# Four gate tiles moved behind the q, k, v projections, sample attention queued by groups, a shared buffer for its value sums, and weight splits on GpSimd beside a convolution

## The chip, the cores and the metric

The kernel runs on one core of a Trainium2 chip. The metric is the device time of one execution in microseconds. Five engines work side by side, each through its own instruction stream in a fixed order: TensorE (PE: matrix products, with PEld for its weight loads), VectorE (DVE), ScalarE (ACT), GpSimd (POOL) and SyncE (SP), which here only issues transfers. An instruction that waits holds up everything behind it on the same engine.

## The reference

One layer of a decoder with two gated branches, on 1024 prompt tokens and 8 sequences of 4 sample tokens, with width 1024 and all in float32:

```
h = RMSNorm(x);  z = h @ w_in -> GLU (2*512) | q, k, v (768 each) | gate_c (1024) | gate_a (1024)
A: GLU -> causal depthwise conv (width 31) -> LayerNorm over channels -> swish -> @ w_conv_out
B: attention in 3 groups of 4 heads, windows/dilations (128,1), (512,4), (2048,16) -> @ w_att_out
x = x + (sigmoid(gate_c) * A + sigmoid(gate_a) * B) @ w_out
x = x + SwiGLU(RMSNorm(x));  x = x + sigmoid(RMSNorm(x) @ w_ple_gate) * (p @ w_ple)
```

The prompt attends to itself. Each sample token attends to 129 or so keys of its sequence's cache (128 kept rows and the new ones) in each group; the caches are also copied to the outputs.

## The kernel before

**Tokens and products.** The 1056 tokens lie along the free dimension in three chunks of 352, features on the 128 partitions. Each large product is float32 made of three products of split operands: `mm3` (L118 to L120) multiplies high by high, high by low and low by high part for each of the 8 tiles along the contraction, so that a tile of 128 output columns for all tokens is 3 x 8 x 3 = 72 matmuls. They are `mm<-...` in the trace.

**Weights.** They come in slabs of 128 x 1024 in the order of a list. `stage` loads a slab (SyncE, L91), `prepare` makes its high part on ACT (`whi`, L101) and its low part on DVE (`wlo`, L102); two slabs are loaded ahead and one is split ahead. A scheduler places each engine's instructions by priority when the program is built; the splits have a raised priority.

**Phase 1** makes the embedding product, the first norm, and then 24 slabs of `w_in`: 8 for the GLU, 8 gate tiles of the conv branch and 8 gate tiles of the attention branch. A gate tile is evacuated from PSUM by ACT's sigmoid (L408) into a tile `et` (two buffers) and stored in DRAM (`gcd`, `gad`). While TensorE works on the gates, DVE makes the depthwise convolution: 31 taps for each of 4 channel tiles, each one operation on 128 x 1024 that reads `U` and `acc` (L332, L338). Then comes the LayerNorm over channels: DVE copies sums and squares of `acc` to `lt` (L366, L367), TensorE sums them over the channels with a matrix of ones (L369), and DVE and ACT normalise and apply swish (L372 to L386). The result is stored as `cd`.

**Phase 2** runs two pairs of heads, each through three groups: q, k and v products, scores (TensorE L707, DVE L712 with the running maxima `mcol`), then softmax and the products with v (L567 to L675). The q, k, v of the sample tokens are written to DRAM (`scr`). Behind pair 1, the pointwise product of the conv branch is made: three chunks of `cd` are loaded in halves into `et` (L758) and split (`split`, L123 on ACT, L124 on DVE), then for each of 8 output tiles the conv gate is loaded into an `et` (L765), three products of 12 matmuls are multiplied by it on DVE (L770) and the result is stored (L771).

**Sample attention** runs beside that, with (query, sequence, head) on the partitions and 8 keys a step. `sample_ops(g)` appends small steps to a queue `bg`. A key step loads 128 x 512 of the cache (L493, tile `kt`, four buffers), multiplies it by the query on GpSimd (L466) and sums over the head's 64 elements on DVE (L467); 16 such steps and one for new keys are followed by the softmax (`smax`). A value step loads the cache, multiplies by the weights on GpSimd (L477), reduces over the 8 keys on DVE (L484) and adds the 128 x 64 result to `oacc` (L487). All three groups are queued behind the conv product's code, and `pump` empties the queue there; the scheduler then interleaves the steps with the prompt's work by data and engine. `sample_out` combines the groups, transposes on TensorE (L516) and writes the sample columns of the attention product's operand (`ohi`, `olo`).

**The attention product** then needs `ohi` and, for each tile and chunk, the gates loaded from `gad` (L795). DVE multiplies its sum by the attention gate (L836), GpSimd adds the conv branch (L837), and the output product L854, the FFN, the embedding gate and the final norm follow.

What sets the order around the change: the slab list, the order of the code with the queue `bg` (and `bga` for softmax steps), and the number of steps that each `pump(n)` takes.

Of the kernel before, what the change touches and what calls it, by code (L numbers as in the profile page):

```python
# [20 lines left out]
TP = 1024            # prompt tokens  # L21
T = 1056             # prompt and sample tokens
NCH = 3              # token chunks
C = 352
CP = (352, 352, 320)  # prompt tokens in a chunk
KD = 8
FT = 22              # tiles of 128 hidden FFN columns
# [4 lines left out]
NB = (8, 8, 8)       # 128-query blocks in a group  # L32
SOFF = (0, 132, 261, 390)

# columns of the "vec" input
# [5 lines left out]
KEPT = (2, 3, 4, 5, 6)   # slabs of the last product that are used twice  # L41
# [3 lines left out]
def hybrid_layer(ctx: ExitStack, tc: tile.TileContext, I, O):  # L45
# [21 lines left out]
    # ---- weights: a slab is up to 8 tiles of 128 x 128, split into two float32r parts.  # L67
    # The slabs come in the order of their use, loads two and splits one ahead. ----
    order = [(I["w_ple"][i], 8) for i in range(2)]
    order += [(I["w_in"][i], 8) for i in range(42)]  # L70
# [13 lines left out]
    keep = [None]        # room for the slabs that are used twice  # L84
    last_act = [None]

# [7 lines left out]
    def prepare():  # L94
        if staged:
            st, n, kept = staged.popleft()
            p, b = (keep[0], len(KEPT)) if kept else (wp, 2)
            hi = p.tile([128, 8, 128], F32R, name="whi", tag="whi", bufs=b)
            lo = p.tile([128, 8, 128], F32R, name="wlo", tag="wlo", bufs=b)
            with tc.high_priority(offset=PRIO):  # L100
                last_act[0] = ac.activation(hi[:, :n, :], st[:, :n, :], AF.Copy)  # L101
                ve.tensor_tensor(lo[:, :n, :], st[:, :n, :], hi[:, :n, :].bitcast(F32), op=OP.subtract)  # L102
            ready.append((hi, lo))
            stage()
# [8 lines left out]
    def mm3(ps, w, ks, rhs):  # L113
        """ps = sum over k of w[k].T @ rhs[k]; ks: slab positions, rhs: (hi, lo) pairs."""
# [11 lines left out]
    def split_gain(hi, lo, x, g):  # L126
        """x times a gain per partition, split"""
        ac.activation(hi, x, AF.Copy, scale=g)
        ve.scalar_tensor_tensor(lo, x, g, hi.bitcast(F32), op0=OP.mult, op1=OP.subtract)

# [32 lines left out]
    J3 = (0, 128, 224)   # three (overlapping) runs of 128 tokens of a chunk  # L163

    def rstd_cols(p, sqs, n=float(D)):
        """1/sqrt(mean + eps) of the tokens of some chunks, tokens on the partitions;
        sqs: squares, summed over the feature tiles (a list: still to be summed)"""
# [11 lines left out]
        # first guess from the bits of v, then three Newton steps  # L179
# [9 lines left out]
    def rstd_rows(cols, i=0):  # L189
        """the same of the i-th chunk, tokens along the free dimension, on every partition (PSUM)"""  # L190
# [19 lines left out]
    # =====================================================================  # L210
    # phase 0 and 1: per-layer embedding product, first norm, gates, conv branch
    # =====================================================================
# [7 lines left out]
    ev = evs.enter_context(pool("ev"))          # evacuation buffers  # L220
# [7 lines left out]
    def mmtile(p):  # L228
        return p.tile([128, 512], F32, name="mm", tag="mm")
# [77 lines left out]
    def proj(evac, psp):  # L307
        """next tile of 128 columns of w_in, for all tokens"""
# [18 lines left out]
    def conv_ops(ct):  # L327
        """depthwise conv of one tile of 128 channels, as a list of small steps"""
# [31 lines left out]
    def layer_norm():  # L360
        """LayerNorm over the channels and swish"""
# [44 lines left out]
    for dst in gc_d + [d[:, 0] for d in ga_d]:  # L406
        et = et_tile()
        proj(lambda c, ps: ac.activation(et[:, c * C:(c + 1) * C], ps[:, :C], AF.Sigmoid), mm1)  # L408
        sy.dma_start(dst, et)
    pump(1000)  # L410
# [5 lines left out]
    # =====================================================================  # L416
    # phase 2: projections to q, k, v and attention, two heads at a time
    # =====================================================================
# [12 lines left out]
    # room for the tiles that are free early is taken last: the next phase's first loads go there  # L431
# [13 lines left out]
    def sample_ops(g):  # L445
# [4 lines left out]
        def load():  # L450
# [3 lines left out]
            st["q"] = a = sp.tile([128, 64], F32, name="sq", tag="sq", bufs=2)  # L454
            sy.dma_start(a, scr[g][0].rearrange("t (h d) -> (t h) d", d=64))
            for i, nm in ((1, "k"), (2, "v")):
                st[nm] = b = sp.tile([128, 4, 64], F32, name="sn" + nm, tag="sn" + nm, bufs=1)
                if g == 0:
                    for j in range(4):
                        sy.dma_start(b[32 * j:32 * j + 32],  # L460
                                     scr[g][i].rearrange("(n b) (h d) -> (b h) n d", n=4, d=64))
                else:
                    sy.dma_start(b[:, 0], scr[g][i].rearrange("t (h d) -> (t h) d", d=64))
# [12 lines left out]
        def v_part(vt, off, n):  # L476
            gp.tensor_tensor(vt, vt, st["s"][:, off:off + n, None].to_broadcast([128, n, 64]), op=OP.mult)  # L477
            if not st.get("o"):
                ve.tensor_reduce(oacc[:, g], vt.rearrange("p n d -> p d n"), axis=AX, op=OP.add)
                st["o"] = True  # L480
                return
            if n > 1:
                pr = sp.tile([128, 64], F32, name="pr", tag="pr", bufs=2)
                ve.tensor_reduce(pr, vt.rearrange("p n d -> p d n"), axis=AX, op=OP.add)  # L484
            else:
                pr = vt[:, 0]
            ve.tensor_tensor(oacc[:, g], oacc[:, g], pr, op=OP.add)  # L487
# [12 lines left out]
        bg.append(smax)  # L500
        steps("v", v_part)

    def sample_out():
# [13 lines left out]
        so = sp.tile([128, 2, 32], F32, name="so")  # L517
# [6 lines left out]
    def group_view(t, g):  # L524
        """prompt columns of t (in group order) seen in natural order: [p, u, r]"""
# [18 lines left out]
    def blocks(g):  # L544
        """(first query, first key, keys, first bias column) of the 128-query blocks"""
# [10 lines left out]
    def softmax_ops(pair, S, VT, mcol):  # L556
        st = {}

        def rows(g, hf):
            """maxima of a group as rows in token order, joined with the groups before"""  # L560
# [121 lines left out]
    for pair in range(2):  # L682
        S, VT = [], []
        mcol = ap_.tile([128, 3, 8, 2], F32, name="mcol", tag="mcol", bufs=2)
        for g in range(3):
# [4 lines left out]
            for i, nm in enumerate("qkv"):  # L690
                t = ap_.tile([128, T], F32, name=nm, tag=nm, bufs=1)
                qkv.append(t)
                proj(lambda c, ps: evac_group(t, g, c, ps, i), psm)
                if i == 1:
                    # scores with bias, and their maxima
# [4 lines left out]
                    for b0 in range(0, 8, 2):  # L700
                        # the two heads lie on different rows of the array: their products alternate
# [16 lines left out]
            # new rows of the caches  # L718
# [8 lines left out]
            # v with tokens on the partitions, and a column of ones for the denominators  # L727
# [11 lines left out]
            # q, k, v of the sample tokens, tokens on the partitions  # L739
            ps = misc()  # L740
            for i in range(3):
# [5 lines left out]
                         st[:, 1:, :])  # L747
        softmax_ops(pair, S, VT, mcol)
        pump(1000, bga)

    # pointwise product of the conv branch and its gate, while the last heads finish
# [20 lines left out]
    for g in range(3):  # L772
        sample_ops(g)
# [5 lines left out]
    # =====================================================================  # L779
    # attention product, gates, output product, first residual; FFN input  # L780
    # =====================================================================
# [32 lines left out]
    def to_input(p, c, m, gain):  # L814
        """the m-th feature tile of x1 to the next product's input (without the token's norm)"""
# [11 lines left out]
    for m in range(KD):  # L827
        if m % 4 == 0:
            w = slab()
        for c in range(NCH):  # L830
            s = slice(c * C, (c + 1) * C)
            ga = ga_next if c + m == 0 else ga_load(c, m)
            ps = mmtile(mm)
# [11 lines left out]
    # the first chunk's input goes to a place of its own, the others' to where their operands were  # L845
# [20 lines left out]
    # =====================================================================  # L866
    # FFN
    # =====================================================================
# [45 lines left out]
    # =====================================================================  # L914
    # PLE gate, last residual, final norm
    # =====================================================================
# [39 lines left out]
def _layout(inp):  # L956
# [12 lines left out]
    def tiles(w):  # L969
        """[K, M] -> [M / 128, 128 rows, K / 128, 128 columns]"""  # L970
# [3 lines left out]
    def slabs(w):  # L974
        """[K, M], K a part of 1024 -> [slab, 128 rows, tiles of a slab, 128 columns]"""
# [41 lines left out]
    # caches with (query, sequence, head) in front: the rows that a query reads  # L1017
# [11 lines left out]
    # constants of the shapes  # L1029
# [41 lines left out]
def _collect(r):  # L1071
# [7 lines left out]
    def prompt(a, n):  # L1079
        # [kv, pair, (e, d), n] in token order -> [n, kv, head, d]  # L1080
# [6 lines left out]
    # new rows: [g, kv, (n, b), (h, d)] -> [g, kv, b, n, h, d]  # L1087
# [4 lines left out]
    for g in (1, 2):  # L1092
        both = []
        for i, n in enumerate("kv"):
            old = r[f"o_{n}g{g}"].reshape(4, 8, 4, 127, 64).transpose(1, 3, 0, 2, 4)   # b, m, i, h, d
# [24 lines left out]
```

## Time and profile before

| | us |
|---|---|
| runs of the kernel before | 1720.19, 1723.10, 1723.71 (median 1723.1) |
| span of the profiled execution | 1721.7 |
| its TensorE busy / DVE / ACT / GpSimd | 1660.9 / 897.6 / 494.4 / 182.7 |

The profile describes one execution; its own time is the span, 1721.7 us, from the first to the last instruction, and the median of the runs is 1.4 us above it. Rows give a line of the kernel, an engine, an operation with the tiles it writes and reads, and times in microseconds unless marked ns; a duration triple is minimum, median and maximum in ns. "Idle before" is time that an engine stood still ahead of an instruction, with what ended the wait.

### The profile page before, as it was taken

Reading aid. Unit: us, or ns where it says so; the run is one execution under the profiler, and the core shown is the slowest. Engines: PE = TensorE matmul, PEld = TensorE weight load, DVE = VectorE, ACT = ScalarE, POOL = GpSimd, SP = SyncE. Lnnn points to the kernel's source line nnn. Section 1 sums busy time; section 2 is a strip of 40 time slices with the busy share of each in tenths; the row PEclk is TensorE's granted clock in tenths of the full one; section 3 lists DMA queues with packets and bytes.
Section 4 is the critical chain, followed back from the end, with each engine's and each line's share of the span. In section 5 each row is a group of like instructions: output and inputs, shape, how many; then the busy total and the mean of one; then the engine's idle time right before and its main releaser. Section 6 shows DMA issues by size and latency. Waiting matters only on the chain.

```text
span 1721.7 us, 25453 instructions
## 1 busy us (share of the span) xinstructions
PE 1660.9 (96%) x10554; PEld 1629.2 (95%) x10554; DVE 897.6 (52%) x1529; ACT 494.4 (29%) x890; POOL 182.7 (11%) x154
## 2 busy tenths in 40 slices
PE   7999999999999978799999999999999999999996
PEld 7999999999998868689999999999999999999996
DVE  7699995121225896874543323333233333337666
ACT  7211125322263225232322201221012111225552
POOL 3100000000003766460000000000000000000003
PEclk9999999999999999899999999999999999999998
DMA  8445554511203678681233323332111111111322
GB/s 306 170 136 172 184 182 156 179 48 55 70 29 116 187 262 269 205 289 50 72 107 120 99 70 99 118 115 74 50 62 37 36 52 62 39 35 51 118 87 108
DMA packets 69348, 201.14 MB, mean 117 GB/s; under 512 B 10096, under 2 KB 25264, under 8 KB 68144
## 3 DMA queue, kind: packets, MB, share of 16 engines
q1 hardware_dynamic: 66480, 153.50, 27.6%
q10 hardware_dynamic: 2752, 46.01, 8.1%
q8 instruction: 83, 1.36, 0.3%
q14 instruction: 33, 0.27, 0.1%
HBM read 171.17 MB, written 72.15 MB: 141 GB/s over the span
## 4 chain that ended last, share of the span: by engine, by line
PE 81%; DVE 6%; issue 6%; DMA 4%; POOL 1%; ACT 1%; SPq 0%; DVEq 0%; POOLq 0%; ACTq 0%
PE mm L118 26%; PE mm L120 25%; PE mm L119 25%; DVE pr L484 2%; DMA kt<-in_kg 2%; PE ps_s L707 1%; PE N L608 1%; POOL kt L466 1%; DVE oacc L487 1%; DMA ga<-gad 1%; DMA et<-gcd 1%; DVE sc L467 1%; PE misc L174 1%; POOL y L922 0%; PE ps_s L631 0%
## 5 line engine op out<-in xcount | busy, mean ns | idle before, releaser
L118 PE MATMUL mm<-hhi,whi 128*128 128x352 f32 x2480 | 807.4, 326 | 13.3 <-DVE et L770 7.7
L120 PE MATMUL mm<-hhi,wlo 128*128 128x352 f32 x2480 | 802.1, 324 | 0.0
L119 PE MATMUL mm<-hlo,whi 128*128 128x352 f32 x2480 | 799.3, 322 | 0.0
L118 PEld LDWEIGHTS mm<-hhi,whi 128*128 128x128 f32 x2480 | 467.2, 188 | 21.1 <-DVE et L770 10.7
L120 PEld LDWEIGHTS mm<-hhi,wlo 128*128 128x128 f32 x2480 | 468.1, 189 | 3.0 <-issue 2.7
L119 PEld LDWEIGHTS mm<-hlo,whi 128*128 128x128 f32 x2480 | 468.5, 189 | 0.6 <-issue 0.2
L101 ACT ACTIVATE whi<-wst 128x1024 fp32r<-128x1024 f32 (+2 forms) x144 | 144.0, 1001 | 463.0 <-PE mm L119 437.6
L102 DVE TENSOR_TENSOR wlo<-wst,whi 128x1024 fp32r<-128x1024 f32 (+2 forms) x144 | 168.5, 1171 | 141.9 <-ACT whi L101 140.3
L118 PE MATMUL mm<-mh,whi 128*128 128x352 f32 x592 | 190.9, 323 | 0.0
L119 PE MATMUL mm<-ml,whi 128*128 128x352 f32 x592 | 189.8, 321 | 0.0
L120 PE MATMUL mm<-mh,wlo 128*128 128x352 f32 x592 | 189.6, 320 | 0.0
L338 DVE SCALAR_TENSOR_TENSOR acc<-U,vec,acc 128x1024 f32<-128x1024 f32 x120 | 147.1, 1277 | 0.4
L908 DVE TENSOR_TENSOR x<-mm,x 128x352 f32<-128x352 f32 x96 | 50.3, 524 | 131.5 <-PE mm L120 131.3
L466 POOL TENSOR_TENSOR kt<-kt,sq 128x512 f32<-128x512 f32 x48 | 64.3, 1366 | 509.9 <-DMA sq<-scr 488.1
L922 POOL TENSOR_TENSOR y<-x,r 128x704 f32<-128x704 f32 x8 | 15.1, 1921 | 923.3 <-ACT r L823 923.3
L119 PEld LDWEIGHTS mm<-ml,whi 128*128 128x128 f32 x592 | 111.2, 188 | 0.0
L118 PEld LDWEIGHTS mm<-mh,whi 128*128 128x128 f32 x592 | 111.1, 188 | 0.0
L120 PEld LDWEIGHTS mm<-mh,wlo 128*128 128x128 f32 x592 | 111.0, 187 | 0.0
L884 DVE TENSOR_TENSOR sg<-mm,r 128x352 f32<-128x352 f32 x66 | 34.5, 524 | 121.9 <-PE mm L120 117.3
L895 DVE TENSOR_TENSOR sg<-mm,sg 128x352 f32<-128x352 f32 x66 | 34.6, 524 | 121.0 <-PE mm L120 121.0
L123 ACT ACTIVATE mh<-sg 128x352 fp32r<-128x352 f32 x66 | 32.5, 493 | 136.2 <-DVE sg L895 136.2
L885 ACT ACTIVATE sg<-sg 128x352 f32<-128x352 f32 x66 | 32.4, 493 | 136.6 <-DVE sg L884 136.3
(170 smaller groups left out, 1327.0 us busy)
## 6 DMA issues: line engine op xcount, KB each, us to landing
o_rest<-in_rest ACTq DMA_DIRECT2D x32, 768.0 KB, 4.8
wst<-in_w_in SPq DMA_DIRECT2D x42, 512.0 KB, 4.8
kt<-in_kg SPq DMA_DIRECT2D x48, 256.0 KB, 3.9
kt<-in_vg SPq DMA_DIRECT2D x48, 256.0 KB, 3.1
wst<-in_w_fg SPq DMA_DIRECT2D x22, 512.0 KB, 3.5
wst<-in_w_fu SPq DMA_DIRECT2D x22, 512.0 KB, 3.6
x<-in_x SPq DMA_DIRECT2D x24, 352.0 KB, 7.2
gad<-et SPq DMA_DIRECT2D x16, 528.0 KB, 4.9
```

Of the source, the lines that this page charges most:

```text
L101: last_act[0] = ac.activation(hi[:, :n, :], st[:, :n, :], AF.Copy)
L102: ve.tensor_tensor(lo[:, :n, :], st[:, :n, :], hi[:, :n, :].bitcast(F32), op=OP.subtract)
L118: te.matmul(ps, hi[:, k, :], rh, start=(i == 0), stop=False)
L119: te.matmul(ps, hi[:, k, :], rl, start=False, stop=False)
L120: te.matmul(ps, lo[:, k, :], rh, start=False, stop=(i == n - 1))
L123: ac.activation(hi, x, AF.Copy)
L338: ve.scalar_tensor_tensor(acc[:, ct, :TP], U[:, ct, j:j + TP], vcol(w0 + j), acc[:, ct, :TP], op0=OP.mult, op1=OP.add)
L466: gp.tensor_tensor(kt, kt, st["q"][:, None, :].to_broadcast([128, n, 64]), op=OP.mult)
L484: ve.tensor_reduce(pr, vt.rearrange("p n d -> p d n"), axis=AX, op=OP.add)
L884: ve.tensor_tensor(sg, ps[:, :C], rT[c], op=OP.mult)
L895: ve.tensor_tensor(sgs[c], ps[:, :C], sgs[c], op=OP.mult)
L908: ve.tensor_tensor(x1[c][:, m], ps[:, :C], x1[c][:, m], op=OP.add)
```

## The change

The changed kernel's line numbers are some higher, and its comments are gone, since the diff also removes them.

- The slab list: 8 GLU slabs, 8 conv gates, 4 attention gates, 18 slabs of q, k, v, and then the other 4 attention gates.
- During the 12 early gates the low part of each weight split is made by GpSimd instead of DVE. Before them and after them DVE makes it.
- The 4 late attention gates are made after pair 1's attention. DVE copies them from PSUM as they are (a sigmoid there is left out), and ACT applies the sigmoid later, to the loaded tile ahead of the attention product.
- `sample_ops(g)` is called when group g of pair 1 is done. `pump(5)` follows each of pair 1's products, `pump(9)` each late gate, `pump(6)` each tile of the conv product.
- A value step's first product goes to a tile `vacc` (128 x 512); each later product is added to it on DVE (`vacc += kt`), and one reduce over the keys at the end makes `oacc`.
- The tiles for the new keys and the new values share one buffer, the one for the query has one buffer instead of two, and `so` takes its place at the end.

```diff
+GA_EARLY = 4
...
-    order += [(I["w_in"][i], 8) for i in range(42)]
+    n_gate = 8 + GA_EARLY
+    order += [(I["w_in"][i], 8) for i in range(8 + n_gate)]
+    order += [(I["w_in"][i], 8) for i in range(24, 42)]
+    order += [(I["w_in"][i], 8) for i in range(8 + n_gate, 24)]
...
-                ve.tensor_tensor(lo[:, :n, :], st[:, :n, :], hi[:, :n, :].bitcast(F32), op=OP.subtract)
+                lo_engine[0].tensor_tensor(lo[:, :n, :], st[:, :n, :], hi[:, :n, :].bitcast(F32),
+                                           op=OP.subtract)
...
-    for dst in gc_d + [d[:, 0] for d in ga_d]:
+    def gate(dst, psp):
         et = et_tile()
-        proj(lambda c, ps: ac.activation(et[:, c * C:(c + 1) * C], ps[:, :C], AF.Sigmoid), mm1)
+        def evac(c, ps):
+            out = et[:, c * C:(c + 1) * C]
+            if psp is mm1:
+                ac.activation(out, ps[:, :C], AF.Sigmoid)
+            else:
+                ve.tensor_copy(out, ps[:, :C])
+        proj(evac, psp)
         sy.dma_start(dst, et)
+    lo_engine[0] = gp
+    for dst in gc_d + [d[:, 0] for d in ga_d[:GA_EARLY]]:
+        gate(dst, mm1)
+    lo_engine[0] = ve
...
-            gp.tensor_tensor(vt, vt, st["s"][:, off:off + n, None].to_broadcast([128, n, 64]), op=OP.mult)
-            if not st.get("o"):
-                ve.tensor_reduce(oacc[:, g], vt.rearrange("p n d -> p d n"), axis=AX, op=OP.add)
...
-                ve.tensor_reduce(pr, vt.rearrange("p n d -> p d n"), axis=AX, op=OP.add)
...
-            ve.tensor_tensor(oacc[:, g], oacc[:, g], pr, op=OP.add)
+            out = vt if st.get("o") else st["acc"]
+            st["o"] = True
+            gp.tensor_tensor(out, vt, st["s"][:, off:off + n, None].to_broadcast([128, n, 64]), op=OP.mult)
+            if out is vt:
+                a = st["acc"][:, :n]
+                ve.tensor_tensor(a, a, vt, op=OP.add)
+        def v_sum():
+            ve.tensor_reduce(oacc[:, g], st["acc"].rearrange("p n d -> p d n"), axis=AX, op=OP.add)
...
                 proj(lambda c, ps: evac_group(t, g, c, ps, i), psm)
+                if pair:
+                    pump(5)
...
+            if pair:
+                sample_ops(g)
         softmax_ops(pair, S, VT, mcol)
         pump(1000, bga)
...
+    for m in range(GA_EARLY, KD):
+        gate(ga_d[m][:, 0], psm)
+        pump(9)
...
         sy.dma_start(ga_d[m][:, 1], et)
-    for g in range(3):
-        sample_ops(g)
+        pump(6)
...
+            if m >= GA_EARLY:
+                ac.activation(ga[:, 0], ga[:, 0], AF.Sigmoid)
```

More of the change, by code (lines that the diff above doesn't have):

```diff
@@ L85, in hybrid_layer @@
     last_act = [None]
+    lo_engine = [ve]
     def stage():
@@ L453, in load, with new_rows @@
             sy.dma_start(st["b"][:, :nk], I["sbias"][:, SOFF[g]:SOFF[g + 1]])
-            st["q"] = a = sp.tile([128, 64], F32, name="sq", tag="sq", bufs=2)
+            st["acc"] = sp.tile([128, CK, 64], F32, name="vacc", tag="vacc", bufs=1)
+            st["q"] = a = sp.tile([128, 64], F32, name="sq", tag="sq", bufs=1)
             sy.dma_start(a, scr[g][0].rearrange("t (h d) -> (t h) d", d=64))
[L456 to L463, printed above, removed]
+            new_rows(1, "k")
+        def new_rows(i, nm):
+            st[nm] = b = sp.tile([128, 4, 64], F32, name="sn" + nm, tag="sn", bufs=1)
+            if g == 0:
+                for j in range(4):
+                    sy.dma_start(b[32 * j:32 * j + 32],
+                                 scr[g][i].rearrange("(n b) (h d) -> (b h) n d", n=4, d=64))
+            else:
+                sy.dma_start(b[:, 0], scr[g][i].rearrange("t (h d) -> (t h) d", d=64))
         def k_part(kt, off, n):
@@ L476, in v_part @@
         def v_part(vt, off, n):
-            gp.tensor_tensor(vt, vt, st["s"][:, off:off + n, None].to_broadcast([128, n, 64]), op=OP.mult)
-            if not st.get("o"):
-                ve.tensor_reduce(oacc[:, g], vt.rearrange("p n d -> p d n"), axis=AX, op=OP.add)
[L480 to L487, printed above, removed]
+            out = vt if st.get("o") else st["acc"]
[6 more added lines that the diff above has]
+            ve.tensor_reduce(oacc[:, g], st["acc"].rearrange("p n d -> p d n"), axis=AX, op=OP.add)
         def steps(nm, part):
@@ L500, in sample_ops @@
         bg.append(smax)
+        bg.append(lambda: new_rows(2, "v"))
         steps("v", v_part)
+        bg.append(v_sum)
     def sample_out():
@@ L516, in sample_out @@
         te.transpose(ps[:64, :128], oacc[:, 0], ident)
-        so = sp.tile([128, 2, 32], F32, name="so")
+        so = sp.tile([128, 2, 32], F32, name="so", tag="sq", bufs=1)
         src = ps[:64, :128].rearrange("d (t h) -> d h t", h=4)
```

## The prediction

> **What bounds the kernel now.** I read the page first: busy shares and the 40 slices.
>
> ```profile
> PE 1660.9 (96%) x10554; PEld 1629.2 (95%) x10554; DVE 897.6 (52%) x1529; ACT 494.4 (29%) x890; POOL 182.7 (11%) x154
> PE   7999999999999978799999999999999999999996
> DVE  7699995121225896874543323333233333337666
> POOL 3100000000003766460000000000000000000003
> ```
>
> TensorE is busy 96% of 1721.7 us; the whole prize is 61 us. Its digits fall below 9 at the ends and in slices 15 to 17 (about 600 to 730 us), where POOL and DVE are busiest: the sample attention. Next the windows of these places, and what TensorE waits for.
>
> ```profile
> 136.00:259.00 123.00, 123.00 (x771) 123.00 (x770) 113.79 (x98) 24.40 (x43) 0.00 (x0) 1.00 0.59 187
> 266.00:331.00 65.00, 65.00 (x412) 64.31 (x412) 24.45 (x55) 31.99 (x51) 0.00 (x0) 1.00 0.61 195
> 533.00:726.00 193.00, 163.68 (x1086) 150.11 (x1085) 154.30 (x289) 64.89 (x134) 118.92 (x102) 0.95 0.71 226
> PE ps_s L707 <- DVE mcol L712: 9.3, 5, 5.9
> PE misc L671 <- DVE rl L664: 8.6, 1, 8.6
> PE mm L118 <- DVE et L770: 7.7, 6, 2.6
> ```
>
> Columns of a window: its length, then busy us and count of PE, PEld, DVE, ACT and POOL, clock, DMA share, GB/s. From 136 to 331 TensorE never rests, though DVE is nearly full up to 259 (conv taps and splits). From 533 to 726 TensorE idles 193 - 163.68 = 29.3 us, and what it waits for are small DVE operations queued behind sample steps. So the change can win at most 29.3 us here, and has a place where it can lose.
>
> **Part 1: the conv stage loses.** Four gates move out of the conv's shadow: a w_in slab is 72 matmuls, and 771 matmuls in 123 us are 0.16 us each, so 11.5 us a gate, 46 us in all. DVE's side of it:
>
> ```profile
> L102 DVE TENSOR_TENSOR wlo<-wst,whi x11: 1211/1226/1226, 136.1 to 251.3; 128x1024 fp32r<-128x1024 f32 x11
>   ACT whi L101: 9.0, 9
> L338 DVE SCALAR_TENSOR_TENSOR acc<-U,vec,acc x81: 1272/1277/1285, 137.2 to 257.7; 128x1024 f32<-128x1024 f32 x81
> 251.28 1.22 DVE L102 TENSOR_TENSOR wlo<-wst,whi 128x1024 fp32r<-128x1024 f32 x1 [0.72 <-ACT whi L101]
> 252.42 6.56 DVE L338 SCALAR_TENSOR_TENSOR acc<-U,vec,acc 128x1024 f32<-128x1024 f32 x5
> 259.01 1.69 DVE L366 TENSOR_TENSOR lt<-acc 128x704 f32<-128x704 f32 x2
> 260.62 0.52 DVE L367 TENSOR_TENSOR lt<-lt 128x352 f32<-128x352 f32 x1
> L369 PE MATMUL misc<-lt,ones x6: 457/458/459, 266.5 to 276.1; 128*128 128x352 f32 x6
> ```
>
> On DVE, before, the splits (L102) stand between the taps (L338):
>
> ```order
> L102 TENSOR_TENSOR wlo<-wst,whi 128x1024
> L338 SCALAR_TENSOR_TENSOR acc<-U,vec,acc 128x1024 x7
> L102 TENSOR_TENSOR wlo<-wst,whi 128x1024
> L338 SCALAR_TENSOR_TENSOR acc<-U,vec,acc 128x1024 x8
> L102 TENSOR_TENSOR wlo<-wst,whi 128x1024
> L338 SCALAR_TENSOR_TENSOR acc<-U,vec,acc 128x1024 x5
> L366 TENSOR_TENSOR lt<-acc 128x704 x2
> ```
>
> The same place on DVE now, the tap being L344 and lt written at L372:
>
> ```order
> L361 TENSOR_REDUCE acc<-win 128x8x4
> L344 SCALAR_TENSOR_TENSOR acc<-U,vec,acc 128x1024 x4
> L362 TENSOR_SCALAR acc<-acc,vec 128x32
> L344 SCALAR_TENSOR_TENSOR acc<-U,vec,acc 128x1024 x70
> L372 TENSOR_TENSOR lt<-acc 128x704 x2
> L373 TENSOR_TENSOR lt<-lt 128x352 x2
> ```
>
> The splits are gone from DVE: it saves 11 x 1.14 (the taps at 252.42 follow the split at 251.28) = 12.5 us and 9.0 us of waits for the ACT half, so the last tap, which ended at 252.42 + 6.56 = 259.0, would end at 237.5. But they run on GpSimd beside the taps, and the trace shows what GpSimd does to such operations:
>
> ```profile
> 1687.71 9.53 POOL L922 TENSOR_TENSOR y<-x,r 128x704 f32<-128x704 f32 x5
> 1689.84 1.92 DVE L943 TENSOR_TENSOR x<-x,sg 128x352 f32<-128x352 f32 x1
> L943 DVE TENSOR_TENSOR x<-x,sg x24: 513/524/1923, 1626.7 to 1707.9; 128x352 f32<-128x352 f32 x24
> L922 POOL TENSOR_TENSOR y<-x,r x8: 1703/1988/2005, 1686.0 to 1699.1; 128x704 f32<-128x704 f32 x8
> L484 DVE TENSOR_REDUCE pr<-kt x45: 998/1064/1097, 568.7 to 720.4; 128x64 f32<-128x512 f32 x45
> L487 DVE TENSOR_TENSOR oacc<-oacc,pr x46: 203/324/1302, 571.2 to 721.5; 128x64 f32<-128x64 f32 x46
> ```
>
> A DVE operation with two SBUF inputs takes 1.92 instead of 0.524 us beside a 128x704 GpSimd one: 1.40 lost. The reduce L484, with one input, never suffers (1.097 at most); the add L487 does. A tap reads U and acc, both in SBUF. Scaled by columns, a 128x1024 split blocks DVE 1.40 x 1024/704 = 2.03 us; at worst for its whole length, 1.703 x 1024/704 = 2.48. No reason excludes 0 if taps and GpSimd interleave better, but the nearest row is L943, so I take 2.03. Eleven of the 12 splits fall among the taps: 22.3 us, last tap at 259.8, lt 2.1 later, as from 259.0 to 261.1 before: 262.0 (rounded up). The Trainium skill, page "SBUF — State Buffer", section "SBUF: two separate sides", calls the port pair of DVE and GpSimd an exclusive lock held for a whole instruction when the DVE operation has two SBUF inputs; L943 agrees, and by it each split would cost up to its full length, the upper value.
>
> TensorE comes to the LayerNorm's first sum earlier now. Before, this stands at its row 1549, in the second chunk of gate 12:
>
> ```order
> L120 MATMUL mm_2216<-hhi_360,wlo_2098 128x352
> L369 MATMUL misc_2757<-lt_2754,ones_70 128x352
> L118 MATMUL mm_2216<-hhi_360,whi_2097 128x352
> L119 MATMUL mm_2216<-hlo_361,whi_2097 128x352
> L120 MATMUL mm_2216<-hhi_360,wlo_2098 128x352
> ```
>
> And now at row 1466, in the first chunk of gate 11:
>
> ```order
> L124 MATMUL mm_2103<-hhi_222,whi_2010 128x352
> L375 MATMUL misc_2409<-lt_2406,ones_70 128x352
> L125 MATMUL mm_2103<-hlo_223,whi_2010 128x352
> L375 MATMUL misc_2429<-lt_2426,ones_70 128x352
> L126 MATMUL mm_2103<-hhi_222,wlo_2011 128x352
> ```
>
> It moved up 83 rows, 13.3 us: from 266.5 to 253.2. Everything behind it on TensorE waits for lt until 262.0: 8.8 us. Before there was no wait, since lt was done at 261.1, 5 us early. The clock dips after such stalls:
>
> ```profile
> 700.00:720.00 20.00, 12.66 (x119) 12.05 (x116) 19.80 (x29) 4.90 (x8) 11.34 (x11) 0.87 0.55 179
> 721.87 1.91 PE L671 MATMUL misc<-ident,rl 128*64 128x128 f32 x8 [8.58 <-DVE rl L664]
> ```
>
> Round a stall of 8.58 the clock averages 0.87: up to 2.6 us of 20, part of it in the idle time itself; I take 1.6. Loss: 10.4 us; 0 without blocking, 15.4 at 2.48 a split. The rest of the LayerNorm lies beside gate 12 and the q products, as it lay beside full TensorE before (65.00 of 65.00). GpSimd has nothing else there, and a gate leaves 11.5 us for a split of 2.5 that is needed one slab later: nothing. ACT's half of the splits is unchanged.
>
> **Part 2: the sample stage gains.** From the last q, k, v of pair 1 (533) to the attention product:
>
> ```profile
> L466 POOL TENSOR_TENSOR kt<-kt,sq x48: 1256/1286/2317, 537.7 to 686.4; 128x512 f32<-128x512 f32 x48
> L477 POOL TENSOR_TENSOR kt<-kt,sc x48: 1037/1043/2026, 566.6 to 716.9; 128x512 f32<-128x512 f32 x48
> L484 DVE TENSOR_REDUCE pr<-kt 128x64 f32<-128x512 f32 x45 | 47.2, 1057 | 0.0
> L487 DVE TENSOR_TENSOR oacc<-oacc,pr 128x64 f32<-128x64 f32 x46 | 22.7, 493 | 0.7
> L124 DVE TENSOR_TENSOR olo<-bcot,ohi x8: 674/689/1107, 512.5 to 726.4; 64x512 fp32r<-64x512 f32 x8
> 725.18 0.66 PE L118 MATMUL mm<-ohi,whi 128*128 128x352 f32 x2 [0.26 <-ACT ohi L123]
> ```
>
> Before, it lasts 725 - 533 = 192; with the four gates 238 for the same work. Three limits:
>
> Floor: TensorE filled throughout, 238 - 29.3 = 209.
>
> Sample chain: the keys of a group (L466) take 566.6 - 537.7 = 28.9 us with their softmax. A value step was 1.057 + 0.493 = 1.55 on DVE. Now it is GpSimd's 1.04 and an add of two SBUF inputs, 0.69 by the 512-column row of L124: overlapped 1.04, exclusive 1.73; I take 1.6, near the upper. The rule named above speaks against this edit: by it the two never overlap, 1.73. So the shared buffer is worth nothing; only the 48 small adds go and 48 larger come. Three key and two value blocks: 5 + 3 x 28.9 + 2 x 16 x 1.6 = 143 us (147 at 1.73).
>
> Conv input: its six cd loads now come after the late gates. SyncE before, in pairs of buffers:
>
> ```order
> L758 DMA et<-cd_92 128x704
> L493 DMA kt<-in_vg 128x512
> L758 DMA et<-cd_92 128x704
> L493 DMA kt<-in_vg 128x512
> L726 DMA o_p<-v 128x1024
> ```
>
> And now, gad_89 being the store of the last gate's tile:
>
> ```order
> L423 DMA gad_88<-et 128x1056
> L514 DMA kt<-in_vg 128x512 x2
> L790 DMA et<-cd_90 128x704
> L96 DMA wst<-in_w_conv 128x1024
> L514 DMA kt<-in_vg 128x512 x2
> L790 DMA et<-cd_90 128x704
> L514 DMA kt<-in_vg 128x512 x4
> L790 DMA et<-cd_91 128x704
> L514 DMA kt<-in_vg 128x512 x3
> L423 DMA gad_89<-et 128x1056
> ```
>
> The last gate's tile holds one of the two et buffers until it is stored, so the loads go through the other one by one (five of six get the same address), each waiting for the split of the one before.
>
> ```profile
> et<-cd SPq DMA_DIRECT2D x6, 352.0 KB, 3.9
> L124 DVE TENSOR_TENSOR hlo<-et,hhi 128x704 fp32r<-128x704 f32 x6 | 6.2, 1046 | 0.0
> L770 DVE TENSOR_TENSOR et<-mm,et 128x352 f32<-128x352 f32 x24 | 12.2, 514 | 2.5 <-DMA et<-gcd 2.5
> et<-gcd SPq DMA_DIRECT2D x8, 528.0 KB, 5.7
> gad<-et SPq DMA_DIRECT2D x16, 528.0 KB, 4.9
> ```
>
> One turn: 3.9 landing, 1.05 on DVE, about as much on ACT and 0.7 of issue and queueing, 6.7 (6.0 without queueing; above 9 if as slow as gad's store and DVE behind a sample step). Five turns: 33.5, to 176.5. Then 8 tiles of 36 matmuls, 5.76 us: 46, to 223. Gain 238 - 223 = 15; the ends 29 (floor) and 2. The 12 copies of raw late gates (L421) are 0.52 us each on DVE (by L770's 0.514, also 352 columns from PSUM); they lie in the chain, 6 us of it among sample steps that leave DVE 39 us free (193 - 154.3): nothing. The 12 sigmoids moved to the attention product lie on ACT, 29% busy: nothing, up to 2 us if DVE's products wait for them. That stage is DVE and GpSimd bound as before.
>
> **Sum.** -15 + 10.4 + 0.5 for the sigmoids = -4.1. The profiled span, 1721.7, is 1.4 below the median of the runs; on the median 1723.1 that is 1719. About 0.2% (3.4 us) is what a measurement of this kernel can tell from no change.
>
> **Rivals.**
> - *Filled to the floor*: gain 29.3, loss 10.4: 1704. For: those 39 free us of DVE. Against: the cd loads in turn.
> - *No blocking at the taps*: the last tap ends at 237.5, ahead of 253.2, no stall: 1709. Against: L943.
> - *Slower*: the conv input comes so late that nothing is won: a turn of 9.2 instead of 6.7 takes 12.5 us, gain 2.5, loss 10.4 to 15.4: 1731 to 1736. It decides from turns of about 8.8, where gain equals loss.
> - *It fills nothing of note*: late gates' copies wait behind sample steps, gain about equal to the loss: 1723.
>
> **How the numbers follow.** Forecast 0.42 (0.22 of it faster, 0.15 within 0.2%, 0.05 slower; alone 1712 to 1727), floor 0.13, no blocking 0.12, slower 0.23, fills nothing 0.10 (0.09 within, 0.01 slower). Faster 0.47, same 0.24, slower 0.29. The range 1702 to 1736 leaves out less than 0.2.
>
> **What would show it.** TensorE idle for 8 to 10 us before L375 near 253; taps (L344) of 3 us where a GpSimd split runs; cd loads (L790) 6 to 7 us apart; attention product about 223 us after pair 1's group 0. Taps all at 1.28 us, or cd loads in pairs, would make it wrong.

## The result, and the profile after

The changed kernel takes 1787.2 us (median of 4 runs, 1786.4 to 1787.5) against 1722.2 for the kernel before: ratio 1.0378, interval 1.0362 to 1.0394. It is slower by 65 us, outside the predicted range of 1702 to 1736. Its profiled span is 1785.7, 64.0 above the span of before.

The page of the changed kernel, busy shares and slices:

```profile
PE 1666.1 (93%) x10554; PEld 1639.0 (92%) x10554; DVE 884.9 (50%) x1483; ACT 488.7 (27%) x886; POOL 297.7 (17%) x166
PE   7998079999999889899999999999999999999996
DVE  7699950422225787546453333333333333336666
POOL 3005942100004777123000000000000000000003
```

TensorE has a new hole: it does nothing in slice 5 (179 to 223 us) and too little in slices 4 and 6. GpSimd is full exactly there, with an operation that is not the sample attention. The waits of TensorE in the changed kernel name it:

```profile
PE mm L126 <- POOL wlo L107: 65.2, 1, 65.2
PE ps_s L732 <- DVE mcol L737: 7.2, 2, 7.0
...
PE mm L125 <- DVE hlo L130: 4.3, 1, 4.3
```

One wait of 65.2 us, for one weight split on GpSimd. GpSimd's own timeline at that place (start, us, engine, operation, idle before):

```profile
136.06 3.37 POOL L107 TENSOR_TENSOR wlo<-wst,whi 128x1024 fp32r<-128x1024 f32 x1 [87.14 <-ACT whi L106]
147.66 2.91 POOL L107 TENSOR_TENSOR wlo<-wst,whi 128x1024 fp32r<-128x1024 f32 x1 [8.23 <-ACT whi L106]
159.30 79.34 POOL L107 TENSOR_TENSOR wlo<-wst,whi 128x1024 fp32r<-128x1024 f32 x2 [8.73 <-ACT whi L106]
250.00 2.40 POOL L107 TENSOR_TENSOR wlo<-wst,whi 128x1024 fp32r<-128x1024 f32 x1 [11.35 <-ACT whi L106]
```

The third and fourth split together last 79.34 us. By the source row below, the longest split took 76.0 us and the middle one of all twelve 2.403, which is its time with nothing in its way. DVE meanwhile, in the same kernel:

```profile
L107 POOL TENSOR_TENSOR wlo<-wst,whi x12: 2385/2403/76017, 136.1 to 331.9; 128x1024 fp32r<-128x1024 f32 x12
135.90 5.80 DVE L344 SCALAR_TENSOR_TENSOR acc<-U,vec,acc 128x1024 f32<-128x1024 f32 x3
155.17 0.23 DVE L362 TENSOR_SCALAR acc<-acc,vec 128x32 f32<-128x32 f32 x1
155.31 22.80 DVE L344 SCALAR_TENSOR_TENSOR acc<-U,vec,acc 128x1024 f32<-128x1024 f32 x19
231.85 7.87 DVE L344 SCALAR_TENSOR_TENSOR acc<-U,vec,acc 128x1024 f32<-128x1024 f32 x3
243.72 1.69 DVE L372 TENSOR_TENSOR lt<-acc 128x704 f32<-128x704 f32 x2
L344 DVE SCALAR_TENSOR_TENSOR acc<-U,vec,acc x120: 1265/1271/3415, 69.0 to 242.4; 128x1024 f32<-128x1024 f32 x120
```

From 155.31 on the taps run with nothing between them, 19 in 22.80 us: 1.27 us each, 1.20 from one start to the next, each beginning just before the one ahead of it ends. Some 60 of them pass, not lengthened, while the third split stands waiting; only among the three taps from 231.85 (7.87 us instead of 3.7) do it and the fourth get in. So this split did not take its turn with DVE: among some 60 taps it got none. The first split did get one. It lasted 3.37 us, 0.97 more than a free one, so it waited for one tap and came in ahead of the next (three taps from 135.90 took 5.80 us instead of 3.7), though those two taps stand as close as the later ones. TensorE stopped at 170, at its first product with the third split's low part, and went on at 235.

Where the 64 us are: the first `scr` store of pair 0 and that of pair 1 cut the run into parts. SyncE's rows of before (L745) and after (L770):

```profile
372.11 0.33 SPq L745 DMA_DIRECT2D scr<-stok  x1
533.35 0.38 SPq L745 DMA_DIRECT2D scr<-stok  x1
L836 DVE TENSOR_TENSOR ga<-mm,ga x24: 509/514/526, 727.9 to 760.7; 128x352 f32<-128x352 f32 x24
```

```profile
395.16 0.33 SPq L770 DMA_DIRECT2D scr<-stok  x1
556.26 0.38 SPq L770 DMA_DIRECT2D scr<-stok  x1
L869 DVE TENSOR_TENSOR ga<-mm,ga x24: 506/512/527, 792.1 to 825.0; 128x352 f32<-128x352 f32 x24
```

The first part ends 23.05 us later although four gates (46.1 us) have left it: a loss of 69.2. Of this 65.2 are the wait, and from 235 to 240 us TensorE's granted clock is 0.50. Between the two stores nothing changes (161.2 and 161.1). The sample stage, up to the attention product's first gate operation, was 727.9 - 533.35 = 194.6 and is 792.1 - 556.26 = 235.8; with the gates' 46.1 that is a gain of 4.9. The rest is unchanged: 69.2 - 4.9 = 64.3.

### The profile page after: what moved, and what is told of

The parts are those of the page before. It is cut to its first block, busy times and chain, and to the rows that moved or that the text cites. A ratio compares the mean times of both kernels' runs of the same rounds, so it can differ in the third digit from the quotient of the medians.

```text
span 1785.7 us, 25449 instructions
## 1 busy us (share of the span) xinstructions
PE 1666.1 (93%) x10554; PEld 1639.0 (92%) x10554; DVE 884.9 (50%) x1483; ACT 488.7 (27%) x886; POOL 297.7 (17%) x166
## 4 chain that ended last, share of the span: by engine, by line
PE 67%; DMA 4%; DVE 4%; POOL 2%; issue 2%; ACT 1%; SPq 0%; DVEq 0%; POOLq 0%; ACTq 0%
PE mm L124 21%; PE mm L126 21%; PE mm L125 21%; DVE vacc L505 1%; DMA kt<-in_kg 1%; PE N L631 1%; POOL kt L489 1%; PE ps_s L732 1%; DMA kt<-in_vg 1%; DMA ga<-gad 1%; PE ps_s L654 1%; POOL kt L502 0%; POOL y L955 0%; PE misc L180 0%; DVE sc L490 0%
## 5 line engine op out<-in xcount | busy, mean ns | idle before, releaser
L126 PE MATMUL mm<-hhi,wlo 128*128 128x352 f32 x2480 | 805.4, 325 | 68.8 <-POOL wlo L107 65.2
L107 DVE TENSOR_TENSOR wlo<-wst,whi 128x1024 fp32r<-128x1024 f32 (+2 forms) x132 | 155.3, 1177 | 99.5 <-ACT whi L106 97.8
L344 DVE SCALAR_TENSOR_TENSOR acc<-U,vec,acc 128x1024 f32<-128x1024 f32 x120 | 153.5, 1332 | 0.4
L107 POOL TENSOR_TENSOR wlo<-wst,whi 128x1024 fp32r<-128x1024 f32 x12 | 104.8, 8735 | 180.6 <-ACT whi L106 180.6
```

The source lines that it names most:

```text
L107: lo_engine[0].tensor_tensor(lo[:, :n, :], st[:, :n, :], hi[:, :n, :].bitcast(F32), op=OP.subtract)
L126: te.matmul(ps, lo[:, k, :], rh, start=False, stop=(i == n - 1))
L344: ve.scalar_tensor_tensor(acc[:, ct, :TP], U[:, ct, j:j + TP], vcol(w0 + j), acc[:, ct, :TP], op0=OP.mult, op1=OP.add)
```

## The experiments

Theory S: the split is starved by back-to-back taps with two SBUF inputs. First rivals: R, the reordered gates or their loads cause the stall; Q, any busy DVE starves GpSimd.

**Splits on DVE again** (`e1_dve_splits`)

```diff
-    lo_engine[0] = gp
```

> The changed kernel with every weight split on DVE again; all else as changed. Theory S (one GpSimd split is starved of the SBUF ports by the back-to-back taps, 65.2 us of TensorE wait, and about 1.6 of half clock after it): that goes, the 11 splits stand among the taps as before, so the last tap ends near 259 and lt near 261 while TensorE is at the LayerNorm's first sum at 253: a new stall of 8 us and 1.6 of clock. 1787 - 67 + 9.5 = 1730. Rival R (the stall came with the reordered gates or the loads of the slabs, not with GpSimd): still near 1787.

Measured: 1731.1 us, ratio 1.0048 (1.0032 to 1.0063) to the kernel before. R falls. The 65 us are gone, and a loss at the LayerNorm is there, but not the expected one. The first sum (L375) stands as far back in TensorE's order as before (1569 matmuls of the trace are ahead of it in both, 1486 in the changed kernel), starts at 265.9 and waits for nothing. The waits come behind it: 3.1 us at L199 for two steps of the normalisation on DVE (1.4 and 1.7; the row below also counts 2.5 from another place), and 5.1 us for the evacuation of q, which on ACT stands behind the LayerNorm's 12 swish operations (L392):

```profile
PE mm L124 <- ACT q L557: 5.7, 2, 5.1
...
PE misc L199 <- DVE nv L192: 4.0, 2, 2.5
286.80 6.96 ACT L392 ACTIVATE acc<-acc,vec 128x352 f32<-128x352 f32 x12 [6.54 <-DVE acc L391]
```

The first `scr` store comes at 336.86, so this part loses 336.86 - (372.11 - 46.1) = 10.8 us; the sample stage, 731.0 - 498.2 = 232.8, gains 7.9. The profile is of one of the shorter of ten executions (1726.5 us; they go from 1725.3 to 1737.0): its span is 3.0 above that of before, the median 7 above, and the rest of the difference is in no profile.

**GpSimd splits in the kernel before** (`e2_before_gpsimd_splits`): `lo_engine` set to GpSimd for the 16 gates, nothing else.

> The kernel before with one edit: the splits during its 16 gates run on GpSimd. Theory S: the taps close ranks as in the changed kernel, the first split that comes in a run of taps without another operation waits until the last channel tile's taps follow one another, some 65 to 76 us; the five gates left over cover the LayerNorm: 1722 + 67 = 1789. Rival R: no stall, within 5 us of 1722.

Measured: 1788.8 us, with the same wait and the same 79.3 us pair:

```profile
PE mm L121 <- POOL wlo L103: 65.2, 1, 65.2
158.26 79.33 POOL L103 TENSOR_TENSOR wlo<-wst,whi 128x1024 fp32r<-128x1024 f32 x2 [8.73 <-ACT whi L102]
```

This edit alone, in one run, makes the whole slowdown.

**Breaks between the taps** (`e3_breaks`)

```diff
                                         acc[:, ct, :TP], op0=OP.mult, op1=OP.add)
+                if (j + ct) % 4 == 0:
+                    ve.tensor_reduce(brk[:, ct:ct + 1], acc[:, ct, 0:8], axis=AX, op=OP.add)
```

> The changed kernel with a tiny DVE reduce (128 x 8 to 128 x 1) behind every fourth tap of a channel tile, which makes a break in the run of taps every 6 to 9 of them; splits stay on GpSimd. Theory S with the finer claim that GpSimd gets the ports at the first DVE operation that does not need them: a split waits 10 us at most (no 76 us one), each takes 2.4 us of the taps' time, last tap near 237.5 + 11 x 2.2 + 4 = 266, a LayerNorm stall of 14 us: 1787 - 67 + 16 = 1736. Rival Q (GpSimd only gets a small share beside any busy DVE): split still tens of us long, 1780 or more.

Measured: 1733.0 us (one run). The longest split is now 6.41 us, and the stall that the prediction had expected appears, 9.1 us at the LayerNorm's first sum:

```profile
158.60 6.41 POOL L107 TENSOR_TENSOR wlo<-wst,whi 128x1024 fp32r<-128x1024 f32 x1 [9.17 <-ACT whi L106]
193.16 2.40 POOL L107 TENSOR_TENSOR wlo<-wst,whi 128x1024 fp32r<-128x1024 f32 x1 [6.98 <-ACT whi L106]
239.24 3.44 POOL L107 TENSOR_TENSOR wlo<-wst,whi 128x1024 fp32r<-128x1024 f32 x1 [8.28 <-ACT whi L106]
228.76 15.01 DVE L345 SCALAR_TENSOR_TENSOR acc<-U,vec,acc 128x1024 f32<-128x1024 f32 x9
PE misc L378 <- DVE lt L376: 9.1, 1, 9.1
L345 DVE SCALAR_TENSOR_TENSOR acc<-U,vec,acc x120: 1268/1276/3424, 69.0 to 261.3; 128x1024 f32<-128x1024 f32 x120
```

Not every split came in at a break. The split of 239.24 came in among nine taps with nothing between them (228.76 to 243.7), after one tap, and so did four others in this run, each between two taps 1.20 us apart. So close taps can shut GpSimd out and do not always do it; what decides is not shown by any run.

Its conv part loses 339.5 - 326.0 = 13.5 us, against 10.8 with the splits on DVE. The 30 breaks take some 3 us of DVE themselves, so the two losses do not rank the engines. Per split GpSimd costs DVE more: eleven taps met a split here and took 2.9 to 3.4 us instead of 1.276, mostly 2.0 to 2.1 lost, where a split on DVE takes 1.14.

**Taps with one input** (`e4_one_input_taps`): each tap is a reduce over one element of `U`; its weight and the running sum are left out.

> The changed kernel with each tap replaced by a reduce over one element of U into acc (one SBUF input of the same 128 x 1024; the tap's weight and the running sum are left out), splits still on GpSimd. Theory S: only operations with two SBUF inputs hold GpSimd off, so every split takes 2.4 us, no tap is lengthened, no stall: 1787 - 69 = 1718. Rival Q: any full DVE starves GpSimd: a split of tens of us, 1780.

Measured: 1717.4 us (one run). DVE was as busy (67.8 of the 68 us from 159 to 227), and while the taps run no split waits:

```profile
158.19 2.41 POOL L107 TENSOR_TENSOR wlo<-wst,whi 128x1024 fp32r<-128x1024 f32 x1 [9.23 <-ACT whi L106]
169.79 2.43 POOL L107 TENSOR_TENSOR wlo<-wst,whi 128x1024 fp32r<-128x1024 f32 x1 [9.19 <-ACT whi L106]
L344 DVE TENSOR_REDUCE acc<-U x120: 1206/1210/1222, 67.9 to 226.5; 128x1024 f32<-128x1024 f32 x120
```

Q falls: DVE's load does not hold GpSimd off. The edit takes away the tap's second SBUF input and changes the kind of operation with it. For the input as the cause speaks the profile of before, where two operations of one kind run beside the same GpSimd operations (L922): the one that reads PSUM and SBUF is not lengthened, the one with two SBUF inputs is. The tap's own kind with a single SBUF input was not run.

```profile
1693.64 0.51 DVE L940 TENSOR_TENSOR sg<-mm,r 128x352 f32<-128x352 f32 x1
1695.69 1.92 DVE L943 TENSOR_TENSOR x<-x,sg 128x352 f32<-128x352 f32 x1
```

**Dependent taps** (`e17_dependent_taps`): the first tap of each channel tile takes its bias from the last tap of the tile before, so that no two taps overlap.

> The changed kernel, splits on GpSimd, with the first tap of each channel tile made to wait for the last tap of the one before, so that every tap follows a tap of its own tile and no two overlap. Theory H (the 0.04 us gap between dependent operations lets GpSimd in): no split over 4 us; the taps take 1.32 us each in place of 1.20 and 2.1 more for each split, last tap near 271, a LayerNorm stall of some 20 us: 1787 - 67 + 21 = 1741. Rival N (only an operation of another kind lets it in): a split of tens of us again, 1787 or more.

Measured: 1744.2 us (one run). No split is longer than 3.43 us; the taps are 1.285 in the middle and start 1.32 apart where no split comes in:

```profile
158.14 3.35 POOL L107 TENSOR_TENSOR wlo<-wst,whi 128x1024 fp32r<-128x1024 f32 x1 [9.25 <-ACT whi L106]
192.94 3.43 POOL L107 TENSOR_TENSOR wlo<-wst,whi 128x1024 fp32r<-128x1024 f32 x1 [9.16 <-ACT whi L106]
L348 DVE SCALAR_TENSOR_TENSOR acc<-U,vec,acc x120: 1268/1285/3509, 67.9 to 274.3; 128x1024 f32<-128x1024 f32 x120
```

Theory H holds: the gap between two dependent taps is enough, and every split waits for one tap at most. In the changed kernel the starvation ends at 233, where the taps begin to start 1.30 to 1.32 us apart as dependent ones do.

**How many gates late** (`e5_no_late_gates`, `e6_two_late`, `e7_three_late`, all with splits on DVE)

```diff
-GA_EARLY = 4
+GA_EARLY = 8   # 6, 5
```

> The changed kernel with splits on DVE and all 8 attention gates early, as before: what is left of the change is the sample attention by groups and the value sums in one buffer. Theory T (the 8 us that the sample stage of the kernel with splits on DVE wins come from the late gates): no gain without them, 1722 to 1727. Rival U (they come from the group order and the shared buffer): 1714 to 1717.

> Splits on DVE, 6 attention gates early and 2 late. TensorE has 23 us more to do before attention than with 4 early ones, against the 10.8 that the LayerNorm cost there: no loss at the conv. Theory T: two late gates fill part of the stage, gain 4 to 8: 1716 to 1720. Theory U: 1714 to 1717, as with none late.

> Splits on DVE, 5 attention gates early and 3 late. 11.5 us more cover against 10.8 us of loss: 0 to 1 at the conv. Theory T: gain 6 to 8, 1716 to 1718. Theory U: 1714 to 1717.

Measured: 1721.1 (ratio 0.9998, 0.9987 to 1.0008), 1732.6 (1.0065, 1.0050 to 1.0080) and 1728.7 (1.0055, 1.0033 to 1.0076). U falls: group order and shared buffer give nothing. T falls too: two or three late gates lose 8 to 12 us. By their profiles (the gates' time taken off as above) the part up to the first `scr` store loses only 0.7 and 2.0 us, so the LayerNorm is nearly covered, but the sample stage, which gains 7.9 with four late gates, loses 6.0 with two and 1.4 with three. Why it does stays open.

**Value sums as before** (`e8_two_late_old_sums`, on the kernel with two late gates)

> Splits on DVE, 2 late gates, and the value sums as before (a reduce of each product, then an add to oacc). Theory V (the shared buffer is worth nothing, since its 128 x 512 adds wait for GpSimd, 1.25 us in the middle where the reduce and the small add took 1.06 and 0.32): within 3 us of the kernel with two late gates. Rival W (the 48 small adds saved count): slower than that by 4 to 8.

Measured: 1732.9 us against 1732.6. The shared buffer is worth nothing that these runs can tell (four of each, 1729.0 to 1735.0); V holds.

**Other buffers for the conv input and the gate tiles** (`e10_cd_buffers`, `e11_cd_gcd_buffers`, `e12_three_late_buffers`, `e13_no_late_buffers`): the places of q, k and v take the conv input, and in all but the first run the conv gate tiles too.

```diff
-            et = et_tile()
+            nm = "qkv"[(2 * c + q) % 3]
+            et = ap_.tile([128, T], F32, name=nm, tag=nm, bufs=1)
```

> Splits on DVE, 4 late gates, and the six cd loads go in turn to the places of q, k and v, which are free by then, instead of the two et buffers that the late gates use. Theory X (behind late gates the conv input comes one load after another through one buffer, and TensorE waits for it): 6 to 10 us less than with splits on DVE alone (1731), 1721 to 1725. Rival Y (the sample steps on DVE and GpSimd set the end of the stage): no change, 1728 to 1734.

> As the kernel with cd loads in the places of q, k and v, and the conv product's gate tiles rotate through those three and the two et buffers. Theory X2 (the gate tile's load, behind its buffer and the ga loads on SyncE, makes the 4 to 6 us of idle near the end of the conv product): 4 to 5 us less than that kernel, 1717 to 1721. Rival Y: no change against it.

> The same two buffer edits with 5 early and 3 late gates, where the LayerNorm is covered to 2 us: theory X says the three late gates then fill idle time: 1728.7 less 10 to 15 = 1713 to 1719, faster than before. Rival Y: 1726 to 1731.

> The same two buffer edits with all gates early: conv input was never late there, only the gate tiles' loads: 0 to 4 us less than without them (1721), 1717 to 1721 under both theories; the control for the kernel with three late gates.

Measured: 1727.4, 1729.5, 1722.0 (ratio 0.9993, 0.9984 to 1.0003) and 1731.3. X holds in part: 4 us with four late gates and 7 with three, less than expected. X2 is not confirmed: 2 us more, not 4 to 5 less. The control misses by 10 us: with no late gates the places of q, k and v come free later than the `et` buffers did, and the last conv split moves from 624 to 663 us. The best of them equals the kernel before.

**Sample attention left out** (`e15_no_sample`, on the kernel with splits on DVE; constants in its place)

> Splits on DVE, 4 late gates, sample attention left out (no key or value steps, constants in their place). Theory Y (sample steps set the stage): nearly all idle of the stage goes but the LayerNorm's 11 us at the conv stays: 1731 less 20 to 28 = 1703 to 1711. Rival Z (the chain of cd loads, gates and softmax sets it by itself): 1720 to 1730.

Measured: 1709.5 us (one run), Y holds. Its stage ends as follows:

```profile
501.87 0.38 SPq L769 DMA_DIRECT2D scr<-stok  x1
L868 DVE TENSOR_TENSOR ga<-mm,ga x24: 510/514/525, 713.2 to 746.3; 128x352 f32<-128x352 f32 x24
```

That is 211.3 us against 232.8 with sample attention: the sample steps cost the stage 21.5.

**Scores first** (`e14_scores_first`, `e16_before_scores_first`): the score operations at the splits' priority.

> Splits on DVE, 3 late gates, cd and gate tiles in the places of q, k, v, and the score operations on DVE with the raised priority of the weight splits, so that they pass the sample steps. Theory P (the 7 us wait of the last group's scores, with its clock dip, is a loss of its own): 1722 less 6 to 11 = 1711 to 1716, faster than before. Rival Y (the sample steps set the end of the stage, so what the scores win the sample loses): 1720 to 1724.

> The kernel before with the score operations on DVE at the splits' priority, nothing else. Theory P: 1723 less 5 to 10 = 1713 to 1718. Rival Y: 1721 to 1725.

Measured: 1723.9 and 1723.1 (ratios 1.0000, 0.9988 to 1.0013, and 0.9994, 0.9982 to 1.0007). Both are inconclusive: in each the wait that the edit was to remove is still there, so P was not put to the test.

```profile
PE ps_s L731 <- DVE mcol L737: 9.1, 3, 6.9
PE ps_s L707 <- DVE mcol L713: 9.8, 5, 6.0
```

## Why the prediction was wrong

**The step that failed** is "Eleven of the 12 splits fall among the taps: 22.3 us, last tap at 259.8". It takes for granted that GpSimd and DVE take turns, with 2.03 us of DVE lost for each turn. The price was right: the slowest tap, 3.415 instead of 1.271, lost 2.14. The turns mostly did not come. The last tap started at 242.4 and ended at 243.7, nearer to the 237.5 of the case without blocking than to 259.8, because only four taps met a split; GpSimd waited in DVE's place, in a split of 76 us, and TensorE behind it, for 65.2. The text weighed 0 and "its whole length" as prices on DVE's side and never priced a split that waits. Its sentence "a gate leaves 11.5 us for a split of 2.5 that is needed one slab later: nothing" is where the bound from above is missing: the order shows 70 taps in one run (`x70`), so that bound is 70 x 1.2 = 84 us, by the distance of 1.20 that the changed kernel shows.

The evidence for turns was L943 beside L922. There at most two DVE operations with two SBUF inputs stand together (L942 and L943); then DVE is idle for some 0.56 us or runs L940, which reads PSUM and was not lengthened. Between the taps there is neither. The Trainium skill, page "SBUF — State Buffer", section "SBUF: two separate sides", says of the shared port pair that whoever starts first keeps it for a whole instruction and the other fully blocks. The runs agree that one engine waits while the other works (a tap of 3.415 us, a split of 76.0), and with the second input as the condition. What they add is that the turn need not pass at the end of an instruction: with taps 1.20 us apart the waiting split missed some 60 such ends, while six other splits, one in the changed kernel and five in the kernel with breaks, came in at the first.

**Conv stage, the other terms.** TensorE's arrival at L375 could not be seen at 253, since it stalled before. The forecast loss was 10.4 (0 to 15.4). With GpSimd's splits and breaks, where the turns come, TensorE arrives at 264.8 - 9.1 = 255.7 and waits 9.1 (forecast 8.8): the mechanism predicted, with a loss of 13.5. With the splits on DVE the loss is 10.8, near the forecast by luck: nothing waits at the first sum there, and the cost is in "The rest of the LayerNorm", which the prediction took to lie beside a full TensorE.

**Sample stage.** Forecast gain 15, measured 4.9 (7.9 with splits on DVE). The conv input was to be complete 176.5 us after pair 1's first store. In the changed kernel, its loads and the last split:

```profile
696.90 0.33 SPq L790 DMA_DIRECT2D et<-cd  x1
702.60 0.33 SPq L790 DMA_DIRECT2D et<-cd  x1
708.19 0.33 SPq L790 DMA_DIRECT2D et<-cd  x1
719.07 0.80 SPq L790 DMA_DIRECT2D et<-cd  x2
725.94 0.33 SPq L790 DMA_DIRECT2D et<-cd  x1
731.39 0.88 DVE L130 TENSOR_TENSOR hlo<-et,hhi 128x704 fp32r<-128x704 f32 x1
```

It was complete at 732.3 - 556.3 = 176.0. The time is right and the turns only in part: the first load came at 140.6 (forecast 143), and the turns were 5.7, 5.6, 10.9, 0.4 and 6.5 us, the fourth and fifth load together, some 5 us after the last late gate's tile was stored (714.27). That the sum fits so well is partly luck. The term that was short is the 46 us for the eight conv tiles; they took to 790, some 58. TensorE was busy for 54.1 of the 58: the last softmax and its products still stood there, and one gate tile came late:

```profile
766.47 0.33 SPq L797 DMA_DIRECT2D et<-gcd  x1
773.20 0.95 DVE L802 TENSOR_TENSOR et<-mm,et 128x352 f32<-128x352 f32 x2 [6.56 <-DMA et<-gcd]
773.78 0.66 PE L124 MATMUL mm<-hhi,whi 128*128 128x352 f32 x1 [3.88 <-DVE et L802]
```

The floor was right as well: forecast 209, and 211.3 without sample attention. So the gain went to the sample steps: they cost 21.5 us, which late gates do not hide. The conv input, now behind the late gates, cost 4 to 7 us by the buffer runs. How the 21.5 us divide among the steps' DVE time, the scores' wait of 7 us and the cache loads stays open.

**Value sums.** "Worth nothing": right (1732.6 and 1732.9). The add took 1.253 us in the middle (673/1253/1771) beside GpSimd's products, between the 1.04 of full overlap and the 1.73 of none.

**The rivals.** The slower one had the right sign for a wrong reason. None let GpSimd be the one that waits. By the prediction's own terms the turn at which gain equals loss is 6.7 + (15 - 10.4)/5 = 7.6 us, not 8.8; nothing else hangs on that.

## What to carry to other kernels

Before work goes from DVE to GpSimd, read in the order what DVE runs at that time. An unbroken run of independent operations with two SBUF inputs can keep GpSimd out for as long as it lasts, and whoever waits for GpSimd pays it all. Bound a shared resource from both sides, for each of the two that share it. A chain that was hidden (here the conv input) must be looked at again when the work that hid it is moved behind it.

## What the runs showed that was not expected

- A 128x1024 subtract on GpSimd (2.40 us free) took 76.0 us while some 60 DVE taps of 1.27 us ran back to back, 1.20 from start to start, unslowed. It came in where the taps began to start 1.30 us apart, as dependent ones do.
- With one DVE reduce of 8 elements every few taps the longest split took 6.4 us, with dependent taps, 1.32 us from start to start instead of 1.20, 3.4. Six splits came in between taps 1.20 apart with no break at that place, so what decides there is open.
- A reduce of the same 128x1024 with one SBUF input, 1.21 us each, delayed GpSimd nothing (2.40 to 2.43 us a split).
